# Sliding-window gather: the last two tiles on other buffers, each stored as one 64-row transfer from SyncE

## Chip, cores, metric

One core of one Trainium2 chip. The metric is the device time of one execution, in microseconds (us); the span is the part of it from the first to the last instruction, as the profile shows it. A transfer has landed when the last of its engines has recorded its completion. A kernel is always timed in rounds beside the kernel before, on the same chip.

## The reference

A batch of 16 images with 64 channels of 64 x 64 floats is cut into 8 x 8 windows at stride 4, so 15 x 15 windows per image overlap by half. There is no arithmetic; it is a copy of 16.8 MB into 59.0 MB (3600 window rows of 16 KB).

```python
# x: (16, 64, 64, 64) float32, window_size 8, stride 4
for i in range(n_h):            # 15
    for j in range(n_w):        # 15
        result[:, i, j] = x[:, :, i*4:i*4+8, j*4:j*4+8]
```

## The kernel before

The input lies in SBUF as `L`: a partition holds 32 channels (half `ch`) of 16 image rows (quarter `hq`) of one image `b`. VectorE (DVE) and ScalarE (ACT) build tiles of up to 128 whole windows in a ring of four buffers `G`, and GpSimd (POOL) sends each tile out with an indirect store, a scatter: each partition's 16 KB row goes to the output row that an index names. Windows that cross from one quarter to the next (`s` = 2 and 3) exist for three quarters only; for these "crossing" scatters the index of 16 partitions is put out of range, and their rows are skipped (GpSimd's queue has 3472 packets of 16 KB in the trace, 240 fewer than 29 x 128).

```python
def tile_():                       # the ring of four
    nonlocal at
    at += 1
    return G[(at - 1) % NG]
...
crossed = 0
def unit(j, s, fast=False):
    nonlocal crossed
    g = tile_()
    if s == 0:
        fill(g, 0, 0, j, 0, HP, (act, dve if fast else shf))
        fill(g, 1, 1, j, 0, HP, (act, dve if fast else mix))
        scatter(g, idx, j, s)
    else:                          # crossing: the two halves take turns
        turn = crossed % 2
        crossed += 1
        fill(g, turn, s, j, 0, HP, (act, act))
        fill(g, 1 - turn, s + 1, j, 0, HP, (shf, mix))
        scatter(g, (idx_hi, idx_lo)[turn], j, s)   # 16 of 128 rows skipped
...                                # 29 scatters; the last is a unit with s == 0
j = NW - 1
tile_()                            # one turn of the ring left out
for s in range(2):                 # the last column of windows: two tiles of 64 rows
    g = tile_()
    cols = slice(j * ST, j * ST + WS)
    for y in range(NY):
        d = slice(QP + y * QP, QP + (y + 1) * QP)      # partitions 32 to 95
        for ch, copy in enumerate((act, dve)):
            f = slice(ch * HP + y * QP, ch * HP + (y + 1) * QP)
            copy(out=g[d, ch*CL:(ch+1)*CL, :, :], in_=L[f, :, s*ST:s*ST+WS, cols])
    g_q = g.rearrange("p c r w -> p (c r w)")
    for q in range(HQ):
        free((nc.sync, nc.scalar)[s * q % 2].dma_start(
            out=o_q[q*NSLOT+s, j], in_=g_q[QP+q : QP+q+(B-1)*HQ+1 : HQ]))
```

`shf` is a shuffle by the identity (a copy made with DVE's shuffle instruction), `mix` splits a copy between ACT and a shuffle, `free` only tells the compiler that stores don't overlap.

Of the kernel before, what the change touches and what calls it, by code (L numbers as in the profile page):

```python
# [10 lines left out]
def kernel(  # L11
# [7 lines left out]
    nc = tc.nc  # L19
    P = nc.NUM_PARTITIONS  # L20

    B, C, H, W = x.shape
    Bo, NH, NW, Co, WSo, WSo2 = out.shape
    WS = int(window_size)
    ST = int(stride)
# [6 lines left out]
    HQ = P // (B * CH)  # L32
    CL = C // CH
    RB = H // HQ
    NSLOT = RB // ST
    NWIN = NH * NW
    CFREE = C * WS * WS
    HP = P // CH
    YB = 8
    NY = B // YB  # L40
    QP = YB * HQ
# [7 lines left out]
    L = lpool.tile([P, CL, RB, W], f32)  # L49
# [71 lines left out]
    o_q = out.rearrange("b i j c r w -> i j b (c r w)")  # L121

    def free(st):
        tc.declare_no_dep(st.ins, group="stores", reason="each store writes rows of its own")
        tc.add_to_no_dep_group("stores", st.ins)
# [27 lines left out]
    act, dve = nc.scalar.copy, nc.vector.tensor_copy  # L153
# [15 lines left out]
    def tile_():  # L169
# [3 lines that stand above are left out]
# [43 lines left out]


    j = NW - 1
    tile_()
    for s in range(2):  # L220
        g = tile_()
        cols = slice(j * ST, j * ST + WS)
        for y in range(NY):
            d = slice(QP + y * QP, QP + (y + 1) * QP)
            for ch, copy in enumerate((act, dve)):
                f = slice(ch * HP + y * QP, ch * HP + (y + 1) * QP)
                copy(out=g[d, ch * CL : (ch + 1) * CL, :, :], in_=L[f, :, s * ST : s * ST + WS, cols])  # L227
        g_q = g.rearrange("p c r w -> p (c r w)")
        for q in range(HQ):
            free((nc.sync, nc.scalar)[s * q % 2].dma_start(out=o_q[q * NSLOT + s, j], in_=g_q[QP + q : QP + q + (B - 1) * HQ + 1 : HQ]))  # L230


# [33 lines left out]
```

## Time and profile before

| | kernel before |
|---|---|
| time, median of 3 first runs | 190.28 us (190.25 to 190.29) |
| time of the profiled execution / its span | 190.74 us / 189.0 us |
| DVE, ACT, POOL busy | 75%, 74%, 25% |
| HBM read, written | 16.78 MB, 62.91 MB as counted (422 GB/s over the span); 3.93 MB more than the output, as much as the 240 skipped rows would hold |

The profiled execution was a slow one: 0.46 us over the median. Spans of single profiles are therefore good to some 0.4 us, and a smaller difference is judged by timed rounds only.

### The profile page before, as it was taken

How to read it: one execution, taken by the hardware profiler on the slowest of the kernel's cores; microseconds unless marked ns; L12 is line 12 of the kernel's file. 1: busy time of each engine (PE TensorE's matmuls, PEld its weight loads, DVE VectorE, ACT ScalarE, POOL GpSimd, SP SyncE). 2: the span in 40 equal slices, each digit the busy share in tenths (PEclk: the TensorE clock that was granted, in tenths of full speed). 3: DMA queues.
4: the chain of work that ended last, by engine and by line, in shares of the span. 5: the costliest groups of instructions: out<-in, count | busy, mean ns of one | idle time of the engine just before them, and what ended most of it. 6: DMA issues, size and time to landing. Idle time of an engine off the chain costs nothing.

```text
span 189.0 us, 557 instructions
## 1 busy us (share of the span) xinstructions
DVE 142.5 (75%) x200; ACT 139.2 (74%) x89; POOL 46.9 (25%) x50
## 2 busy tenths in 40 slices
DVE  4000009999697979799989999999999999997410
ACT  0000009998699999988889999999999999974740
POOL 7321212207217170522220222222222222223000
DMA  4999999999999999999999999999999999999993
GB/s 118 308 409 397 402 401 397 397 403 394 427 434 420 435 434 416 434 434 413 437 437 408 439 430 420 423 437 416 427 413 434 428 409 430 406 437 378 427 389 153
DMA packets 11044, 75.81 MB, mean 401 GB/s; under 512 B 3344, under 2 KB 3344, under 8 KB 7440
## 3 DMA queue, kind: packets, MB, share of 16 engines
q0 software_dynamic: 8784, 65.81, 84.0%
q1 hardware_dynamic: 2048, 8.91, 12.0%
q10 hardware_dynamic: 208, 1.05, 1.8%
q14 instruction: 4, 0.03, 0.0%
HBM read 16.78 MB, written 62.91 MB: 422 GB/s over the span
## 4 chain that ended last, share of the span: by engine, by line
DMA 66%; DVE 18%; issue 6%; ACT 3%; POOL 2%; DVEq 0%; ACTq 0%; PEldq 0%
DMA out_dram<-G,idx_hi 24%; DMA L<-in_x_dram 23%; DMA out_dram<-G,idx 13%; DVE G L158 10%; DMA out_dram<-G,idx_y 7%; DVE G L151 5%; DVE G L181 3%; ACT G L227 2%; POOL L L58 2%; ACT G L148 1%; DVE G L148 0%; DVEq L181 0%; POOL pi L69 0%; DVEq L158 0%; PEldq L261 0%
## 5 line engine op out<-in xcount | busy, mean ns | idle before, releaser
L148 ACT COPY G<-L 64x2048 f32<-64x2048 f32 x46 | 87.2, 1896 | 5.5 <-DMA out_dram<-G,idx 2.3
L181 DVE COPY G<-L 32x2048 f32<-32x2048 f32 x30 | 36.6, 1221 | 29.3 <-DMA L<-in_x_dram 26.7
L158 DVE STREAM_SHUFFLE G<-L 64x1024 f32<-64x1024 f32 (+3 forms) x40 | 55.7, 1392 | 1.3
L151 DVE STREAM_SHUFFLE G<-L 64x1024 f32<-64x1024 f32 x30 | 38.5, 1282 | 0.0
L181 ACT COPY G<-L 32x2048 f32<-32x2048 f32 x18 | 33.9, 1896 | 2.9 <-DMA L<-in_x_dram 2.3
L181 ACT ACT_TABLE_LOAD x1 | 1.3, 1283 | 28.3 <-DMA L<-in_x_dram 28.3
L58 POOL DMA_DIRECT2D L<-in_x_dram x16 | 10.9, 691 | 23.0 <-DMA L<-in_x_dram 22.5
L128 POOL DMA_INDIRECT out_dram<-G,idx_y x6 | 10.0, 1664 | 25.5 <-DVE G L181 24.5
L128 POOL DMA_INDIRECT out_dram<-G,idx x8 | 11.3, 1412 | 19.9 <-DVE G L158 6.5
L128 POOL DMA_INDIRECT out_dram<-G,idx_hi x8 | 7.7, 963 | 30.7 <-DVE G L151 23.1
L128 POOL DMA_INDIRECT out_dram<-G,idx_lo x7 | 6.7, 961 | 27.5 <-DVE G L151 19.1
L227 ACT COPY G<-L 32x2048 f32<-32x2048 f32 x4 | 7.6, 1896 | 5.1 <-DMA out_dram<-G,idx_lo 4.0
L162 ACT COPY G<-L 64x256 f32<-64x256 f32 (+1 forms) x20 | 9.1, 456 | 0.5
L227 DVE COPY G<-L 32x2048 f32<-32x2048 f32 x4 | 4.9, 1219 | 3.5 <-DMA out_dram<-G,idx_hi 2.4
L148 DVE COPY G<-L 64x2048 f32<-64x2048 f32 x6 | 7.3, 1222 | 0.2
L158 DVE LOAD_MASK_SELECT G<-L x40 | 0.4, 9 | 2.1 <-DMA out_dram<-G,idx_y 1.2
L72 DVE TENSOR_SCALAR tb<-pi 128x1 int32<-128x1 int32 x1 | 0.2, 153 | 1.0 <-POOL pi L69 1.0
L78 DVE TENSOR_TENSOR th<-tc,tq 128x1 int32<-128x1 int32 x2 | 0.3, 156 | 0.0
L75 DVE TENSOR_SCALAR th<-tc 128x1 int32<-128x1 int32 x2 | 0.3, 154 | 0.0
L69 POOL IOTA pi<- 128x1 int32 x1 | 0.1, 124 | 0.4 <-PEq L261 0.4
L151 DVE LOAD_MASK_SELECT G<-L x30 | 0.2, 7 | 0.0
L78 DVE CUSTOM_DVE_ANT_0 idx_lo<-tb,th 128x2 uint16<-128x2 uint16 x1 | 0.2, 159 | 0.0
(18 smaller groups left out, 2.6 us busy)
## 6 DMA issues: line engine op xcount, KB each, us to landing
L<-in_x_dram SPq DMA_DIRECT2D x8, 896.0 KB
L<-in_x_dram POOLq DMA_DIRECT2D x6, 1024.0 KB, 21.6
L<-in_x_dram POOLq DMA_DIRECT2D x2, 768.0 KB, 18.3
out_dram<-G SPq DMA_DIRECT2D x6, 256.0 KB
L<-in_x_dram POOLq DMA_DIRECT2D x8, 128.0 KB, 21.6
L<-in_x_dram ACTq DMA_DIRECT2D x1, 512.0 KB
out_dram<-G ACTq DMA_DIRECT2D x2, 256.0 KB
out_dram<-G,idx POOLq DMA_INDIRECT x8, 12.3
```

The costliest lines, as they stand in the source:

```text
L58: eng.dma_start(out=L[p0 : p0 + QP - HQ + 1 : HQ, c0:c1, :, :], in_=x_v[ch, y, q, :, c0:c1, :])
L69: nc.gpsimd.iota(pi[:, :], pattern=[[0, 1]], base=0, channel_multiplier=1)
L72: nc.vector.tensor_scalar(out=d[:, :], in0=pi[:, :], scalar1=shift, scalar2=mask, op0=ALU.logical_shift_right, op1=ALU.bitwise_and)
L75: nc.vector.tensor_scalar(out=d[:, :], in0=a[:, :], scalar1=float(m), scalar2=None, op0=ALU.mult)
L78: nc.vector.tensor_tensor(out=d[:, :], in0=a[:, :], in1=b[:, :], op=op)
L128: st = nc.gpsimd.indirect_dma_start(out=o_v, out_offset=bass.IndirectOffsetOnAxis(ap=ix[:, 0:1], axis=0), in_=g.rearrange("p c r w -> p (c ...
L148: copy(out=g[d, cs, :, :], in_=L[f, :, s * ST : s * ST + WS, cols])
L151: nc.vector.stream_shuffle(out=g[d, cs, ST:WS, :], in_=L[f, :, 0:ST, cols], mask=nxt)
L158: nc.vector.stream_shuffle(out=out, in_=in_, mask=same)
L162: act(out=out[:, 0:k], in_=in_[:, 0:k])
L181: (act if (2 * d + ch) % 3 == 0 else dve)(out=g[d * QP : (d + 1) * QP, ch * CL : (ch + 1) * CL, :, :], in_=L[f : f + QP, :, s * ST : s * S ...
L227: copy(out=g[d, ch * CL : (ch + 1) * CL, :, :], in_=L[f, :, s * ST : s * ST + WS, cols])
```

## The change

The intent: let the final tiles be filled earlier (no turn of the ring left out), share out their copies so that DVE, the faster copier (1.22 us against ACT's 1.90 for a 32x2048 copy, L181), takes more, and replace eight stores of 16 rows from two queues by two stores of 64 rows from one.

```diff
     j = NW - 1
-    tile_()
+    half_c = CL // 2
     for s in range(2):
         g = tile_()
         cols = slice(j * ST, j * ST + WS)
-        for y in range(NY):
+        for y, ch, c0, c1, copy in (
+            (0, 0, 0, CL, act),
+            (0, 1, 0, CL, dve),
+            (1, 0, 0, half_c, act),
+            (1, 1, 0, CL, dve),
+            (1, 0, half_c, CL, dve),
+        ):
             d = slice(QP + y * QP, QP + (y + 1) * QP)
-            for ch, copy in enumerate((act, dve)):
-                f = slice(ch * HP + y * QP, ch * HP + (y + 1) * QP)
-                copy(out=g[d, ch * CL : (ch + 1) * CL, :, :], in_=L[f, :, s * ST : s * ST + WS, cols])
-        g_q = g.rearrange("p c r w -> p (c r w)")
-        for q in range(HQ):
-            free((nc.sync, nc.scalar)[s * q % 2].dma_start(out=o_q[q * NSLOT + s, j], in_=g_q[QP + q : QP + q + (B - 1) * HQ + 1 : HQ]))
+            f = slice(ch * HP + y * QP, ch * HP + (y + 1) * QP)
+            copy(
+                out=g[d, ch * CL + c0 : ch * CL + c1, :, :],
+                in_=L[f, c0:c1, s * ST : s * ST + WS, cols],
+            )
+        g_q = g.rearrange("p c r w -> p (c r w)")[QP : QP + B * HQ]
+        free(nc.sync.dma_start(out=o_q[s::NSLOT, j].rearrange("q b f -> b q f"), in_=g_q))
```

## The prediction

> **What bounds the kernel now.** I read the page's slices and queues first. The change touches only the last 17 us of 189, so the question is what those are limited by.
>
> ```profile
> DVE  4000009999697979799989999999999999997410
> ACT  0000009998699999988889999999999999974740
> DMA  4999999999999999999999999999999999999993
> GB/s 118 308 409 397 402 401 397 397 403 394 427 434 420 435 434 416 434 434 413 437 437 408 439 430 420 423 437 416 427 413 434 428 409 430 406 437 378 427 389 153
> ```
>
> The DMA row is 9 in 38 of 40 slices, also where the copy engines have gaps. The 16 transfer engines are the bound nearly to the end; only what lets one of them go empty can cost time, and only filling such a gap can save any. So I cut the end into stretches (columns: length, DVE, ACT, POOL, clock, DMA share, GB/s).
>
> ```profile
> 60.00:168.00 108.00, 103.32 (x151) 101.85 (x69) 25.68 (x23) 1.00 1.01 425
> 168.00:174.00 6.00, 4.95 (x5) 1.99 (x3) 2.45 (x2) 1.00 1.01 423
> 174.00:175.00 1.00, 1.00 (x1) 0.98 (x2) 0.09 (x1) 1.00 0.58 246
> 175.00:181.50 6.50, 2.64 (x3) 5.31 (x3) 0.00 (x0) 1.00 1.03 436
> 181.50:184.50 3.00, 0.00 (x0) 0.00 (x0) 0.00 (x0) 1.00 0.91 377
> 184.50:186.50 2.00, 0.00 (x0) 0.00 (x0) 0.00 (x0) 1.00 0.66 279
> 186.50:189.00 2.50, 0.00 (x0) 0.00 (x0) 0.00 (x0) 1.00 0.00 0
> ```
>
> All that is lost: 0.42 us at 174 to 175 (1 minus 0.58), 0.27 at 181.5 to 184.5 (3 times 0.09), 0.68 at 184.5 to 186.5 (2 times 0.34), together 1.37 us of mean engine time. The 2.5 us after the last byte are waiting for the landing and the program's end, which the change keeps. The timeline shows who feeds the queues then:
>
> ```profile
> 168.17 0.96 POOL L128 DMA_INDIRECT out_dram<-G,idx_hi  x1 [3.80 <-ACT G L148]
> 169.90 1.85 DVE L158 STREAM_SHUFFLE G<-L 64x1536 f32<-64x1536 f32 x1
> 172.51 1.58 POOL L128 DMA_INDIRECT out_dram<-G,idx  x1 [3.38 <-issue]
> 172.70 3.81 ACT L227 COPY G<-L 32x2048 f32<-32x2048 f32 x2 [3.99 <-DMA out_dram<-G,idx_lo]
> 172.75 2.45 DVE L227 COPY G<-L 32x2048 f32<-32x2048 f32 x2 [1.00 <-DMA out_dram<-G,idx_lo]
> 176.54 7.58 SPq L230 DMA_DIRECT2D out_dram<-G  x6
> 177.59 3.81 ACT L227 COPY G<-L 32x2048 f32<-32x2048 f32 x2 [1.07 <-DMA out_dram<-G,idx_hi]
> 177.60 2.47 DVE L227 COPY G<-L 32x2048 f32<-32x2048 f32 x2 [2.41 <-DMA out_dram<-G,idx_hi]
> 181.44 2.19 ACTq L230 DMA_DIRECT2D out_dram<-G  x2
> ```
>
> The ring has four buffers. Both final tiles wait for the scatter that last read their buffer: the first until 172.7, the second until 177.5. Their eight small stores are issued from 176.54 to 184.1; the last of them only when the first tile's bytes are long under way.
>
> [...] The ScalarE queue has 208 packets: a load of 16 x 8 rows (128) plus 16, and two stores of 16 rows plus 16 each: 144 + 64 = 208. SyncE's has 2048: eight loads of 8 x 28 rows plus 8 (1856), six stores at 32 (192). So the 16-row stores used 16 engines, one 16 KB row each. [...] a scatter's issue takes 0.96 us beside shuffles, but the one at 172.51 takes 1.58, ending 0.12 us after the first copy from 172.75 (1.22 us, to 173.97). The one at 68.45, issued inside a copy, takes 2.50 and ends 0.12 after the second copy:
>
> ```profile
> 68.38 3.70 DVE L181 COPY G<-L 32x2048 f32<-32x2048 f32 x3 [1.05 <-DMA out_dram<-G,idx_y]
> 68.45 2.50 POOL L128 DMA_INDIRECT out_dram<-G,idx  x1 [1.00 <-ACT G L148]
> ```
>
> [...]
>
> **The change part by part.** Buffers: the skipped turn of the ring is gone, so the final tiles take the buffers of the fourth- and third-last scatters, not those of the third- and second-last. The first of these (issued at 158.66) should land near 168, since scatters take 9.3 us there (163.41 to 172.67, 168.17 to 177.51); the second lands at 172.67. The first tile thus waits for no transfer, only for its copy engine.
>
> Copies: ACT does 1 full and 1 half copy per tile, 1.90 + 0.95 = 2.85 us; DVE 2 full and 1 half, 1.22 + 1.22 + 0.62 = 3.06 plus gaps of 0.03, 3.12. DVE ends the last scatter's tile at 171.75, so it fills the first final tile until about 174.9 (ACT until 171.6), and the second from there to 178.0 (ACT, 172.7 to 175.6). Before, ACT's two copies made these 176.51 and 181.41. The stores go out at 174.95 and 178.1 instead: the first 1.6 us earlier, the last complete one (before: issue ended at 184.13) about 5 us earlier, allowing 1.3 us of issue.
>
> Stores: 8 of 256 KB become 2 of 1 MB. The sides are 64 rows against 16 x 4 rows[...]. Bytes and rows per engine are the same, only 96 completion writes go (8 x 16 to 2 x 16). At 426 GB/s over 16 engines a 16 KB row takes 0.616 us per engine; the work is equal.
>
> What it costs: the last scatter is issued at 172.51 as before, because its tile isn't touched. But DVE's copies now start at 171.77, so the issue falls inside one (to 172.99) and by the pattern above ends 0.12 us after the second: 174.22 + 0.12 = 174.34 against 174.09. That scatter refills the engines that ran empty at 174: the hole gets 0.25 us longer for those then empty, some 60%, so +0.15 us of mean share. [...]
>
> What it saves: with all 64 rows of the second tile queued by 179.5, no engine lacks work from 181.5 on: -0.27 us. The 0.68 in the last two microseconds is partly late rows and partly engines that end at different times. The two kinds of crossing scatter skip 16 rows each, and a row is 0.6 us, so some stagger stays; I give the change half, -0.34.
>
> Sum: +0.15 - 0.27 - 0.34 = -0.46, and 190.28 - 0.46 = 189.8; I put 189.9, since an engine that ends last may not have been among the starved. Check from the other side: the second-last scatter landed at 177.51, about 1.2 us after its last byte if the final stores' landing is a guide (the queue's wait ends near 187.6, last bytes at 186.5), so its slowest engine was busy until about 176.3. It then has 8 rows of the last scatter and 8 of the stores, 16 x 0.616 = 9.86: 186.2. The last byte came at 186.5, so that engine can win only 0.3. Both ways the gain is under half a microsecond, 0.2%.
>
> **Rivals.** (a) *The tail was an issue bottleneck*: eight issues at 1.3 us and late fills. Then the whole loss after 181.5 and part of the hole return: about -1.0 us, 189.3. For it: the last fill ended at 181.4 and the share falls just there. Against: 1.03 share until then, and the per-engine account. (b) *Descriptor starvation*: DVE copies run back to back from 171.8 to 178, and GpSimd might lose more than one turn; each turn more is 1.25 us, with up to 60% of the engines empty: +0.4 to +0.8, 190.7 to 191.0. For it: 2.50 us issues exist. Against: in none of the seven early scatters was more than two copies' time lost. (c) *The two-sided shape costs the spread*: if 64 rows against 16 x 4 went to only 4 engines, 2 MB at a quarter of 426 GB/s would take 19.7 us from 176: near 199, slower by 4%. [...] (d) *Nothing*: the slowest engine decides and never starved: 190.3.
>
> **Range and chances.** My account gives 189.9; (a) reaches 189.3, (b) 190.7; the range takes these in, 189.2 to 190.8. Faster by 2% needs 186.5, more than all the lost 1.37 us: 1%. Slower by 2% needs 194.1, only (c): 3%. Within 2%: 96%.
>
> **What would show it.** Right: final copies of DVE start near 171.8, the first store goes out near 175 and the second near 178, SyncE's queue has 2016 packets (1856 + 2 x 80) and ScalarE's 144; the last scatter's issue takes about 1.83 us; DMA share stays at 1.0 from 175.5 to 184.5 and the last byte lies at 186.0 to 186.3. Wrong: an issue over 2.5 us (rival b), a store on few engines with a long low-share tail (c), or a first store that waits for a buffer after all. A last byte before 185.6 would mean that I undervalued late issue (a).

What it reads from the queues is in the trace's packet records: SyncE's queue has 160 completions of 4 bytes, 8 from each of eight loads and 16 from each of six stores, and 96 rows of 16 KB. That the scatter's issue waits for the end of DVE's fp32 copies is called the lock theory below; before the result it rested on the issues of 0.96, 1.58 and 2.50 us alone.

## More of the kernel before

Each engine ends with a few closing instructions that the profile calls DRAIN; they stand behind the DMA queues here. The DMA queues (packets, MB, share of 16 engines' time); queue 1 is SyncE's and queue 10 ScalarE's:

```profile
q1 hardware_dynamic: 2048, 8.91, 12.0%
q10 hardware_dynamic: 208, 1.05, 1.8%
```

By line (count, shortest/median/longest ns, first and last start in us):

```profile
L261 POOLq DRAIN  x3: 51/105/12829, 172.3 to 188.7; - x3
L261 SPq DRAIN  x3: 7/7/7, 188.1 to 188.4; - x3
```

GpSimd's first closing drain starts at 172.3, when its last scatter is only being handed over, and takes 12.8 us: it ends at 185.1, three microseconds before SyncE gets to its own at 188.1.

## The result, and the profile after

190.88 us median of 6 runs (190.12 to 191.16) against 190.28 (190.11 to 190.60, 6 runs). The ratio is 1.0025 with a 95% interval of 1.0006 to 1.0044. A ratio is as the timing program gives it; it is not quite the ratio of the medians (1.0032). The changed program was timed twice more among the experiments: 1.0008 (0.9994 to 1.0022) and 1.0004 (0.999 to 1.0018). So it is no faster; it is equal or up to a quarter of a percent slower.

The same stretches of the changed kernel (length, DVE, ACT, POOL, clock, DMA share, GB/s):

```profile
168.00:174.00 6.00, 5.90 (x5) 4.96 (x4) 2.40 (x2) 1.00 1.03 434
174.00:175.00 1.00, 0.97 (x2) 0.97 (x2) 0.43 (x1) 1.00 0.43 180
175.00:181.50 6.50, 3.13 (x4) 0.56 (x1) 0.00 (x0) 1.00 0.99 418
181.50:184.50 3.00, 0.00 (x0) 0.00 (x0) 0.00 (x0) 1.00 1.01 426
184.50:186.50 2.00, 0.00 (x0) 0.00 (x0) 0.00 (x0) 1.00 0.60 254
```

This view counts a transfer whole in the stretch where it starts. By it the hole at 174 grew from 0.42 to 0.57 us, the loss at 181.5 to 184.5 (0.27) is gone, and the loss at 184.5 to 186.5 rose from 0.68 to 0.80; two more profiles of the same program (below) give 0.42 and 0.45 for the hole and 0.72 and 0.96 for the tail, so differences of 0.1 to 0.2 are within its scatter. From the packets' own start and duration the hole (174 to 176) grew from 0.35 to 0.51 or 0.52 us in all three. The timeline, the queues and the closing instructions:

```profile
168.97 2.96 ACT L232 COPY G<-L 32x2048 f32<-32x2048 f32 x2 [0.35 <-DMA out_dram<-G,idx_hi]
...
171.83 6.37 DVE L232 COPY G<-L 32x2048 f32<-32x2048 f32 x6
172.57 1.86 POOL L128 DMA_INDIRECT out_dram<-G,idx  x1 [3.38 <-ACT G L232]
...
175.09 3.76 SPq L237 DMA_DIRECT2D out_dram<-G  x2
```

```profile
q1 hardware_dynamic: 2016, 9.44, 12.6%
q10 hardware_dynamic: 144, 0.52, 1.1%
```

```profile
L268 POOLq DRAIN  x3: 51/105/16053, 172.3 to 188.9; - x3
L268 SPq DRAIN  x3: 7/7/7, 187.5 to 188.7; - x3
```

Up to the stores everything is as worked out: the copies start at 171.83, the issue takes 1.86 us, the stores go out at 175.09 and 178.26, the packets are 2016 and 144. SyncE is done at 187.5, 0.6 us earlier than in the profile of before (the slow one). But GpSimd's drain now takes 16.05 us and ends at 188.4. SyncE waits for it, and the end (189.19) is about where it was (188.96).

The trace's completion records say why. The last scatter's sixteen engines reported until 183.23 before and until 186.51 after; the last store's until 187.61 before and 187.13 after. Against that profile the stores are earlier by half a microsecond and the scatter is later by 3.3, because the stores' rows now run beside the scatter's from 177.0 on (before: from 180.0). The half microsecond must not be taken for a gain of the change. In the profile of before the end comes 1.35 us after the last store's landing; a run at the median, with a span of 188.5, would have it near 187.15 (an estimate from these numbers), and the changed kernel's three profiles have 187.13 to 187.32. From 177 to 180, 58 rows began on GpSimd's queue and 22 on SyncE's (before: 73 and 2, by the packets' records), and with the first store behind (experiment e5) the same scatter lands at 182.20.

**Theories.** *GpSimd theory*: the program ends 0.8 us after the later of two things, SyncE's last wait (0.4 to 0.5 us after the last store has landed) and GpSimd's drain (1.89 us after the last scatter has landed); the change moved the end from the first to the second. *Descriptor rival*: DVE's early copies lengthen the scatter's issue and the hole at 174, and that is the cost. *Last-landing rival*: only the last landing of any queue counts. A further question is why the losses that did go away bought nothing.

### The profile page after: what moved, and what is told of

Same layout as the page of the kernel before. It is cut to its first block, busy times and chain, and to the rows that moved or that the text cites. A ratio compares the mean times of both kernels' runs of the same rounds, so it can differ in the third digit from the quotient of the medians. Undisturbed runs are those within 1.5% of the kernel's fastest.

```text
span 189.2 us, 552 instructions
## 1 busy us (share of the span) xinstructions
DVE 143.9 (76%) x202; ACT 137.5 (73%) x89; POOL 46.4 (25%) x50
## 3 DMA queue, kind: packets, MB, share of 16 engines
q1 hardware_dynamic: 2016, 9.44, 12.6%
## 4 chain that ended last, share of the span: by engine, by line
DMA 57%; DVE 27%; issue 7%; POOL 2%; ACT 1%; DVEq 1%; PEldq 0%; ACTq 0%
DMA L<-in_x_dram 23%; DVE G L158 14%; DMA out_dram<-G,idx 14%; DMA out_dram<-G,idx_hi 13%; DMA out_dram<-G,idx_y 7%; DVE G L151 7%; DVE G L232 3%; DVE G L181 3%; POOL L L58 2%; ACT G L148 1%; DVE G L148 0%; DVEq L268 0%; DVEq L181 0%; POOL pi L69 0%; DVEq L158 0%
## 5 line engine op out<-in xcount | busy, mean ns | idle before, releaser
L181 DVE COPY G<-L 32x2048 f32<-32x2048 f32 x30 | 36.6, 1221 | 29.5 <-DMA L<-in_x_dram 26.5
L181 ACT COPY G<-L 32x2048 f32<-32x2048 f32 x18 | 33.9, 1896 | 3.2 <-DMA L<-in_x_dram 2.3
L128 POOL DMA_INDIRECT out_dram<-G,idx x8 | 10.7, 1337 | 19.9 <-ACT G L148 9.6
L232 ACT COPY G<-L 32x2048 f32<-32x2048 f32 (+1 forms) x4 | 5.9, 1470 | 1.1 <-DMA out_dram<-G,idx_lo 0.7
L232 DVE COPY G<-L 32x2048 f32<-32x2048 f32 (+1 forms) x6 | 6.2, 1041 | 0.2
```

What stands on the lines that cost most here:

```text
L128: st = nc.gpsimd.indirect_dma_start(out=o_v, out_offset=bass.IndirectOffsetOnAxis(ap=ix[:, 0:1], axis=0), in_=g.rearrange("p c r w -> p (c ...
L181: (act if (2 * d + ch) % 3 == 0 else dve)(out=g[d * QP : (d + 1) * QP, ch * CL : (ch + 1) * CL, :, :], in_=L[f : f + QP, :, s * ST : s * S ...
L232: copy(out=g[d, ch * CL + c0 : ch * CL + c1, :, :], in_=L[f, c0:c1, s * ST : s * ST + WS, cols],)
```

## The experiments

Each kernel was run in five rounds beside the kernel before; spans and landings are those of its one profile. Ratios are to the kernel before, with the 95% interval; all but e4's count as the same by the 2% rule, so small differences are read with the intervals and the traces.

**e1, the buffers alone**: the kernel before without the skipped turn.

```diff
-    tile_()
     for s in range(2):
```

> The kernel before with only the skipped turn of the ring taken out: eight small stores, copies as before. First fill by 174.3, stores trickle out from then at about 1.35 us each, so the last scatter shares the engines with them, though with fewer rows at once than in the changed kernel. GpSimd theory (the program ends when GpSimd's closing drain ends, 1.89 us after the last scatter has landed, if that is later than the last store's landing plus about 0.5): scatter lands near 185.5, GpSimd's drain ends near 187.4, span 188.2 to 188.8. Rival, the last landing of any transfer alone decides: span 188.3 to 188.6. Rival, the early fill itself costs (the DVE copies lengthen the last scatter's issue, and the hole at 174 to 175 grows): span 189.2 or more.

Measured: ratio 0.9995 (0.9981 to 1.0008), span 188.8, at the upper edge of the range. The scatter landed at 185.64 and GpSimd's drain ended at 187.53, both as expected; SyncE came later, at 188.00. The issue was 1.86 us here too, and the span is not over 189.2, which speaks against the descriptor rival.

**e2, the merged stores alone**: the kernel before with the skipped turn and its own copies.

```diff
-        for q in range(HQ):
-            free((nc.sync, nc.scalar)[s * q % 2].dma_start(...16 rows...))
+        free(nc.sync.dma_start(out=o_q[s::NSLOT, j].rearrange("q b f -> b q f"), in_=g_q[QP : QP + B * HQ]))
```

> The kernel before with its skipped turn and its copies, but each final tile stored in one transfer of 64 rows. Stores go out at 176.55 and 181.45. GpSimd theory: the first store's 64 rows are all there by about 177.5 [...], so the last scatter lands near 184.5 to 185 (before 183.2), its drain ends near 186.8, still under the last store's path: span 188.7 to 189.0, equal to before. Rival, the large store is itself slower than four small ones: span over 189.3.

Measured: 0.9991 (0.9977 to 1.0005), span 188.4. The scatter landed at 183.53, a microsecond before the expectation (how the store and the scatter share the engines, on which that number rested, was an assumption, not shown by a trace), and the drain ended at 185.42. The span is under the range given (188.7 to 189.0), which had been set from the slow profile. The large store is not slower. Neither part alone shows a loss of time. The early fills alone already delay the scatter by 2.4 us (185.64 in e1 against 183.23), the merged stores alone by 0.3; with both it lands at 185.8 to 186.5.

**e3, an attempt to hold the first store back**: the two stores written in reversed order after both fills.

```diff
-        free(nc.sync.dma_start(...))
+        held.append((o_q[s::NSLOT, j].rearrange("q b f -> b q f"), g_q))
+    for o, g_q in reversed(held):
+        free(nc.sync.dma_start(out=o, in_=g_q))
```

> The changed kernel with its first store held back until the second tile is filled (both issued from about 178.2). Nothing else moves; the last scatter's issue stays at 1.86 us. GpSimd theory: the last scatter has the engines to itself until about 179.3, lands at 181 to 183, its drain ends by 185; the stores land near 187.1 as in the changed kernel and the end follows 1.3 us later: span 188.3 to 188.6, time 0.3 to 0.8 us under the changed kernel's and a little under that of before. Rival (the longer issue and the bigger hole at 174 to 175 made the changed kernel slow): these stay, so span 189.1 or more, since a held store can only lengthen the hole.

This test failed: the compiler's scheduling restored the order, and the trace shows the same instructions on every engine as the changed kernel's. It counts as a repeat of it: ratio 1.0008, span 188.7, scatter landed at 185.98, drain ended at 187.87 (again 1.89 after), later than SyncE's 187.58.

**e4, the last scatter as two plain stores** from partitions 0 to 63 and 64 to 127.

```diff
-            scatter(g, idx, j, s)
+            if plainly:                     # only for the last tile
+                for h in range(2):
+                    g_h = g.rearrange("p c r w -> p (c r w)")[h * HP : (h + 1) * HP]
+                    free(nc.sync.dma_start(out=o_q[h::NSLOT, j].rearrange("q b f -> b q f"), in_=g_h))
```

> The changed kernel with its last scatter made into two plain stores of 64 rows from SyncE, so that GpSimd has nothing in flight after 177.4. GpSimd theory: its drain ends near 179.3 and no copy of DVE lies in the way of an issue; the first half is issued near 171, the second near 172.5, the hole at 174 to 175 closes, the last landing comes near 186.7 and the end 1.3 us after: span 187.8 to 188.2. Rival, the transfer engines' own stagger and total bytes set the end and the closing drain costs nothing: span 188.6 to 189.1.

Measured: 1.0255 (1.0241 to 1.0269), 5 us slower, which no theory had. The stretches show engines that are busy but move less:

```profile
168.00:172.00 4.00, 3.93 (x4) 3.93 (x4) 0.95 (x1) 1.00 0.99 414
172.00:180.00 8.00, 5.84 (x6) 2.96 (x3) 0.00 (x0) 1.00 1.00 287
180.00:188.00 8.00, 0.00 (x0) 0.00 (x0) 0.00 (x0) 1.00 0.99 320
```

The rate fell from 414 to 287 GB/s at a share of 1.00. The two new stores differ from those of the final tiles, which have the same form, in their partitions (0 to 63 and 64 to 127 against 32 to 95; those moved 418 GB/s beside the scatter in the changed kernel, at 175 to 181.5), but no run here changes the partitions alone, so the cause is not shown. GpSimd's drain was out of the way (186.2, 1.85 after its last landing), but the test says nothing of the theories: the change that it makes besides is much larger than what it was to tell apart.

**e5, the first store really behind the second**, by an order edge between the two.

```diff
-        free(nc.sync.dma_start(...))
+        stores.append(nc.sync.dma_start(...))
+        free(stores[-1])
+    tc.add_manual_dep(stores[0].ins, stores[1].ins.name,
+        mybir.DependencyInfo(mybir.DependencyClass.NoSync, mybir.DependencyReason.DATA), ...)
```

> The changed kernel with the first store really put behind the second in SyncE's queue (the earlier try to hold it was undone by the compiler's scheduling). GpSimd theory, with its formula from the traces so far: the end is the later of last store's landing plus 1.3 and last scatter's landing plus 2.65. Both stores go out from 178.25; the scatter has the engines to itself from 175.4 to about 179.3 and lands at 182 to 183.5; the stores land near 187.1 as before; span 188.3 to 188.6, against 189.2 and 188.7 in the two profiles of the changed kernel's program. Rival, the later issue of the last scatter and the larger hole are what cost: they stay, span 188.7 to 189.4.

Measured: 0.9992 (0.9979 to 1.0005), span 188.3. The closing instructions:

```profile
L271 POOLq DRAIN  x3: 51/105/12091, 172.0 to 188.0; - x3
L271 SPq DRAIN  x3: 7/7/7, 187.5 to 187.8; - x3
```

The scatter landed at 182.20 and the drain ended at 184.1, while the issue (1.84 us) and the hole at 174 stayed. The landing of the last store (187.07) is that of the changed kernel. So the order of the queues moved the drain by 4 us with nothing else touched, as the GpSimd theory has it, and what the descriptor rival blames stayed without costing time. In time the difference is small (0.9992 here; 1.0025, 1.0008 and 1.0004 for the changed program), and these are rounds of different calls.

**e6, the scatter last**: the final tiles are made and stored before the last scatter's tile.

```diff
     while plain:
         ...
+        if len(plain) == 1:
+            break
         unit(*plain.pop(0))
     ...                       # the two final tiles
+    unit(*plain.pop(0))
```

> The changed kernel with its two final tiles made and stored ahead of the last scatter, so that the scatter is the last transfer to land; no fp32 copy of DVE runs beside its issue. GpSimd theory: the scatter is issued near 179, lands near 187.0 and the end follows 2.65 later: span 189.5 to 189.9, the time over the changed kernel's by about 0.5, although the hole at 174 to 175 closes and the last byte comes no later. Rival, what counts is the last landing by whatever queue: span 188.2 to 188.5.

Measured: 1.006 (1.0047 to 1.0073), span 190.1.

```profile
L270 POOLq DRAIN  x3: 51/105/10558, 178.8 to 189.8; - x3
L270 SPq DRAIN  x3: 7/7/7, 187.9 to 189.6; - x3
```

The scatter landed at 187.44, the drain ended at 189.32, 1.88 later, and the end followed at 190.12. The last landing is within 0.2 us of that of before (187.61, a store), but the span is over a microsecond longer: the last-landing rival (188.2 to 188.5) is out. This is the run that shows the drain as a cause; the timed rounds agree, 1.2 us over before. The span is a little over the range that I gave, since DVE's copies now lay beside the scatter before, whose issue took 1.86 us, and 0.46 us were lost again at 180 to 182.

**e7, no fp32 copy beside the issue**: DVE's first copy of the first final tile by a shuffle.

```diff
-            (0, 1, 0, CL, dve),
+            (0, 1, 0, CL, shf if s == 0 else dve),
```

> The changed kernel with DVE's first copy of the first final tile (the one that the last scatter's issue falls into) done by a shuffle with the identity, 2.4 us instead of 1.22. Lock theory of the prediction: the issue takes 0.97 instead of 1.86, ends at 173.5 instead of 174.4, and the loss at 174 to 176 (0.52 us of mean engine time) falls to 0.1 to 0.2; the first store goes out 1.2 us later, near 176.3, so the scatter lands 1 to 1.5 us earlier, near 185.0, and by the GpSimd formula the end is then set by the stores: span 188.0 to 188.4. Rival, the issue's length is not due to DVE's copies: it stays at 1.86 and the span at 188.7 or more.

Measured: 0.999 (0.9977 to 1.0003), span 188.6. The issue, and the stretches with the hole and the end:

```profile
172.31 0.96 POOL L128 DMA_INDIRECT out_dram<-G,idx  x1 [3.38 <-ACT G L232]
```

```profile
174.00:175.00 1.00, 0.97 (x1) 0.98 (x2) 0.00 (x0) 1.00 1.07 442
...
184.50:186.50 2.00, 0.00 (x0) 0.00 (x0) 0.00 (x0) 1.00 0.48 205
```

The lock theory holds: with one fp32 copy made a shuffle, the issue takes 0.96 us and not 1.86, and the hole is closed. (An issue that began inside a copy waited for the end of the next copy too where copies ran back to back: in the kernel before the one at 68.45 took 2.50 us, in the changed one that at 172.57 took 1.86, to 0.14 us after the second copy's end.) The descriptor rival is answered once more, since without the long issue and the hole the span is that of the changed kernel's repeats (188.66 and 188.54). But the span missed its expected range (188.0 to 188.4), because the idle time only moved: the loss at 184.5 to 186.5 went from 0.80 to 1.04 us. The engines that run empty at 174 are not the ones that end last. In the kernel before, the share from 174.5 to 175 is 0.50 by the packets' records, with 8 packets in flight against 16 up to 174.1: eight of sixteen engines are empty. The completions of the last store come in two groups of eight as well: in the changed kernel their medians are 185.62 and 186.95, here 184.54 and 186.89. The early group ends a microsecond sooner, the late one where it was. By the packets' own start and duration, 0.52 us at 174 to 176 and 0.35 at 184 to 186 in the changed kernel became 0.05 and 0.88 here.

**e8, the crossing scatters start with the other half.**

```diff
-    crossed = 0
+    crossed = 1
```

> The changed kernel with the crossing scatters starting with the other half (7 of the first kind and 8 of the second instead of 8 and 7), same bytes. Stagger theory: the 16 completions of a scatter come in two groups of eight; after the one at 168.2 they lie 2.1 us apart (174.8 and 176.7 on), since each crossing scatter gives one half of the engines two rows less (1.23 us) and there is one more of the one kind. Flipped, the gap there closes to 0 to 0.5, the loss at 174 to 176 and after 184 falls, last landing near 186.6, span about 0.4 to 0.6 under the changed kernel's. Rival, the half that lags is fixed by the loads and the skipped rows do not add up: gap and span as in the changed kernel, 188.7 to 189.2.

Measured: 189.36 us median, ratio 0.9957 (0.9938 to 0.9976), span 187.5, more than expected (the gap between the groups closed less than expected, to 0.98 us).

```profile
174.00:175.00 1.00, 0.97 (x2) 0.98 (x2) 0.00 (x0) 1.00 0.95 393
...
184.50:186.50 2.00, 0.00 (x0) 0.00 (x0) 0.00 (x0) 1.00 0.18 74
186.50:187.50 1.00, 0.00 (x0) 0.00 (x0) 0.00 (x0) 1.00 0.00 0
```

The completions of every scatter come in two groups of eight. In the kernel before, the first group ends at 174.83 and the second at 177.51 for the crossing scatter issued at 168.17; here they end at 175.49 and 176.47. A crossing scatter skips 16 rows; if they fall on one group of eight engines, that is two each, 1.23 us at 0.616 us a row (in the trace of before a packet of 16 KB takes 0.613 in the median). There are fifteen such scatters: with eight of one kind and seven of the other, one such step is left over. The traces show the steps: the medians of the two groups lie 2.06 us apart at the last scatter ahead of the crossing ones (issued at 78.22), then 3.21, 1.92 and 3.13 after the first three crossing scatters, and 2.59 after the last; each of the fifteen moves it by 1.13 to 1.34 us, a plain scatter among them by less than 0.1. In e8 it is 2.10, then 0.81, 1.96 and 0.78, and 0.66 after the last. So in the kernel before the step left over adds to a lead that the same engines have anyhow; flipped, it takes most of that lead back. The lead is there in the first scatter of all (2.40), so it is older than any skipped row; where it comes from is open. A candidate in the record, not tested: each of SyncE's eight loads has eight completions and not sixteen, and its queue has 8 load packets in flight for 24 us of the 39 with any and never over 10, so it seems to run on half of the engines. The last store landed at 186.27 and SyncE was done at 186.66; the drain (185.70) was no longer the last. Two of the six runs took 190.1 and 190.2 all the same (called slow in an expectation below).

**The changed kernel again, and the flip in the other two forms.** The next three compare directly. e9 is the kernel before with `crossed = 1` alone; e10 is the changed kernel with both the flip of e8 and the order edge of e5.

> The changed kernel once more, beside the next two. GpSimd theory: the last scatter lands between 185.9 and 186.6, GpSimd's drain ends 1.89 after it and is the last thing to end but for the 0.75 of the closing handshake; span 188.6 to 189.2, ratio to before 1.000 to 1.003. If the scatter lands before about 185.5 in this profile, the stores set the end and the span is near 188.4.

> The kernel before with nothing but the first crossing scatter on the other half (the 8 and 7 of the two kinds exchanged). Stagger theory: as in the changed kernel, the two groups of engines come together after the scatter at 168.2, nothing is lost at 174 to 176, and about 1 us is won: span 187.7 to 188.1, ratio 0.994 to 0.997. Starvation by late small stores, if it is real once the engines are level, would show here and not in the flipped changed kernel: then the span stays over 188.3 with a loss at 180 to 184 above 0.3.

> The changed kernel flipped and with the first store behind the second. GpSimd theory: in the flipped changed kernel the drain (185.70) was already under SyncE's last wait (186.6), so putting the store behind wins nothing more: span 187.3 to 187.7, ratio 0.994 to 0.997, drain near 184. If late landings of the scatter made the two slow runs (190.1 and 190.2) of the flipped changed kernel, this one has none of them: all runs under 189.6.

| kernel | time, median (runs) | ratio to before, 95% interval |
|---|---|---|
| changed, again | 190.38 us (190.22 to 190.86) | 1.0004, 0.9990 to 1.0018 |
| e9, before + flip | 189.64 us (189.41 to 189.84) | 0.9963, 0.9951 to 0.9975 |
| e10, changed + flip + edge | 189.20 us (189.13 to 189.25) | 0.9937, 0.9924 to 0.9950 |

The changed kernel's scatter landed at 185.82, a little earlier than the range I gave, the span (188.54) is just under its range, and drain and SyncE ended together at 187.71. e9's span (187.62) is just under its range too; its profile lost 0.09 us at 180 to 184, so late small stores starved nobody in it. That profile is of e9's fastest run. e10 had no run over 189.25. That fits the idea that e8's two slower runs were late scatters, but neither was profiled, so it isn't shown. No run of e10 overlaps one of e9: with level engines and the first store held behind, the change is worth 0.44 us in the medians. SyncE's shorter waits are 0.13 of it (table below); the rest has no cause shown. e10 is the best version found, 0.6% under the kernel before, still within the 2% called the same.

All profiles but e4's, from the traces' completion and instruction records, in us:

| kernel | last scatter landed | GpSimd drain ended | last store landed | SyncE done | end |
|---|---|---|---|---|---|
| before | 183.23 | 185.12 | 187.61 | 188.13 | 188.96 |
| changed | 186.51 | 188.40 | 187.13 | 187.52 | 189.19 |
| e3 (same program) | 185.98 | 187.87 | 187.19 | 187.58 | 188.66 |
| changed again | 185.82 | 187.71 | 187.32 | 187.71 | 188.54 |
| e1 | 185.64 | 187.53 | 187.48 | 188.00 | 188.83 |
| e2 | 183.53 | 185.42 | 187.19 | 187.58 | 188.41 |
| e5 | 182.20 | 184.09 | 187.07 | 187.46 | 188.29 |
| e6 | 187.44 | 189.32 | 182.57 | 187.87 | 190.12 |
| e7 | 184.29 | 186.18 | 187.34 | 187.73 | 188.56 |
| e8 | 183.81 | 185.70 | 186.27 | 186.66 | 187.49 |
| e9 | 181.33 | 183.22 | 186.27 | 186.79 | 187.62 |
| e10 | 181.32 | 183.21 | 186.21 | 186.60 | 187.43 |

Drain minus scatter is 1.88 or 1.89 in every row. The end minus the later of columns 3 and 5 is 0.79 to 0.83 in every row. SyncE minus store is 0.39 with two stores and 0.52 with eight (in e6 SyncE waits for the scatter).

## Why the prediction was right or wrong

- **The bound**: right. The last byte comes 1.5 to 3.0 us before the end in all forms but e4 (packet records), and the changed kernel's time stayed within 0.3%. One reading was off: the stretches count a transfer where it starts, so the last byte before came at 187.0, not at 186.5, and the end 1.9 us after it, not 2.5.
- **Fills, issue times, the spread over 16 engines, packet counts, the longer issue**: right, each to within 0.2 us (ACT's first fill came later); 1.86 us against 1.83 for the issue, 2016 and 144 packets exactly, 16 completions for each of the two stores. The first store's first row began 1.9 us after its issue (177.02 against 175.09). Rivals (b) and (c) did not happen. Rival (d), that the slowest engine decides and never starved, came nearest.
- **The hole, +0.15**: right as idle time (0.35 to 0.51 or 0.52 by the packets), though half of the engines were empty and not "some 60%", a number that no line shown gives. **Starvation at 181.5 to 184.5, -0.27**: right as idle time (to nothing in all three profiles). As time, neither term counted: e7 filled the hole, and only the early engines ended sooner.
- **The tail, -0.34**: wrong in size and sign. It measured +0.12 (+0.04 and +0.28 in the repeats), so in the first profile the three terms together gave about 0 and not -0.46. The "stagger" named there is most of it: eight engines end 1.0 to 1.3 us before the others, and work given to them sooner only lets them end sooner (2.35 us before the others in e7; in e8 it is 0.55). A share averaged over 16 engines was counted as time, which it is only for the engine that ends last. The check from the other side, which followed that engine, said at most 0.3 us and was the better one; the last store landed 0.3 to 0.5 us earlier in three profiles of the changed program, but against a profile of before that was itself 0.46 us slow, so a gain is not shown.
- **The step that failed outright**: "The 2.5 us after the last byte are waiting for the landing and the program's end, which the change keeps." It keeps them only while a store lands last by a margin. The stores queued earlier delayed the last scatter by 2.6 to 3.3 us, and its path to the end, 1.89 + 0.8 us, is 1.4 to 1.5 us longer than a store's, 0.4 or 0.5 + 0.8. In the three profiles of the changed program the drain ended 0.88, 0.29 and 0.00 us after SyncE; that is what it cost there. That the order among transfers of equal total size matters was not in any rival.
- **Range**: 189.2 to 190.8 held the scaled time (1.0025 x 190.28 = 190.76) only just, at its far side from the forecast gain; the plain median, 190.88, lies just above it. That side of the range had been opened for rival (b), which did not happen, so that it held was luck. The later calls gave 1.0008 and 1.0004: no difference from before, and no gain.

What stays open: where the lead of eight engines before the crossing scatters comes from, and why the changed program's times spread over 1 us in the first rounds (190.12 to 191.16); the scatter's landing, which varied from 185.8 to 186.5 in three profiles, explains a part of it. Open too is why e10 beats e9 by more than SyncE's shorter waits.

## What to carry to other kernels

When transfers bound the end, write down for each queue when its last transfer lands and what its engine still does afterwards; here the end was the largest sum, not the last byte. Let the queue with the longest closing path (here GpSimd's, 1.4 to 1.5 us longer) land first, and hold back transfers that would share the engines with it (in e5 the scatter landed at 182.20 so, not at 186.51). And before filling idle time, find whose it is: here, filling the idle time of the engines that lead bought nothing, while levelling them (here one changed constant) bought 0.4%.
